# Two-layer trunk on one core: the memory tokens' keys and values computed in one pass over the contraction, with the keys a step behind

## The chip, the cores and the metric

The kernel runs on one core of one Trainium2 chip. The metric is the device time of one execution in microseconds (us); the time before is the median of three runs. Engines are named as the profile names them: PE (TensorE), PEld (its weight loads), ACT (ScalarE), DVE (VectorE), POOL (GpSimd) and SP (SyncE, which issues most of the DMAs).

## The reference, cut to what matters

Two layers (L = 2), 256 tokens, model width 2048, 256 memory tokens, float32. Each layer makes one input projection of `x`, runs three groups of heads on it, gates and concatenates them, projects the result and normalises. The change touches the part that reads the memory:

```
mkv = mem @ w_mem_kv                      # (256 x 2048) @ (2048 x 1024)
mk, mv = jnp.split(mkv, 2, axis=-1)       # keys and values, 512 columns each
...
y_m = memory_attention(heads_m(m_q), heads_m(mk), heads_m(mv))
...
return layer_norm(DEEPNORM_ALPHA * x + out, ln_g, ln_b)
```

`mem` is the same in both layers; `w_mem_kv` is not. The second layer's `x` is the first layer's result.

## The kernel before, in words

**Products in three parts.** Every float32 operand is split into a high part (ACT casts it to fp32r, line 117) and a low part (DVE subtracts, line 118); the helper `parts` does both. A product takes high·high, low·high and high·low. A cast therefore goes DMA, then ACT, then DVE, and PE needs all three.

**Pieces and quarters.** The contraction over 2048 is cut into 16 blocks of 128. Activations come in four *quarters* of 4 blocks (512 KB each; `load_quarter`, tile `x` from the pool `opp` with 5 buffers). Weights come in *pieces* of 512 KB (`piece`, tiles `raw`, `wh`, `wl`, 4 buffers each).

- `as_group` keeps the activations stationary and streams the weights: a piece is 2 blocks by 512 columns, 12 products of 512 columns. The memory's values (`G_MV`) are made so, in 8 pieces.
- `ws_group` keeps the weights stationary and streams the activations: two halves, each 4 pieces of 4 blocks by 256 columns, 16 products per piece (8 of 512 columns, 8 of 256). The memory's keys (`G_MK`) are made so, in 8 pieces that go over all four quarters twice; then the queries and keys of group B (`G_BQK`) from `x`.

**Order.** PE and SP follow the order in which the code is written (`manual_schedule`). ACT, DVE and POOL are ordered by a scheduler at build time; each then works strictly in that order. A pool gives a tile a buffer when its first writer is placed, in the order of the tiles. The heads are generators that `tick()` advances after each piece; the number that a generator yields is how many ticks it rests.

**The start of layer 0.** `begin_pieces` loads the memory's first two quarters and the first four pieces of the values in slices, all on SP's queue and all in `raw` buffers. Memory quarters 2 and 3 follow with `load_quarter`; the four quarters of `xT` are loaded inside `G_BQK`. The tile `res` (the residual, 2 MB) is not written before SP loads `xn` into it, after the second group of values of the heads.

**The start of layer 1.** `transposed` turns the residual into the four quarters of `x`, on PE: 8 groups of 4 transposes, one group after every second tick, each followed by a cast (ACT) and a subtraction (DVE) from a PSUM bank. It starts after the eight value pieces; `finish` runs off what is left. The memory's quarters of layer 1 are loaded and cast while the layer before is still in its output projection.

Of the kernel before, what the change touches and what calls it, by code (L numbers as in the profile page):

```python
# [8 lines left out]
F32 = mybir.dt.float32  # L9
F32R = mybir.dt.float32r  # L10
# [6 lines left out]
DVE = mybir.EngineType.DVE  # L17

P = 128
D = 2048  # L20
T = 256
# [11 lines left out]
G_MK, G_MV, G_BQK, G_AQ0, G_AK0, G_AQ1, G_AK1, G_MQ, G_BZ, G_AZ0, G_AZ1, G_MZ, G_WO = range(13)  # L33
AHEAD = 4000
# [3 lines left out]
def hybrid_trunk_kernel(  # L38
# [7 lines left out]
    pe, dve, act, pool, sp = nc.tensor, nc.vector, nc.scalar, nc.gpsimd, nc.sync  # L46
# [42 lines left out]
    def nm(s):  # L89
        uid[0] += 1  # L90
        return f"{s}_{uid[0]}"

    def mm(o, l, r, start, stop):
        pe.matmul(o, l, r, start=start, stop=stop, skip_group_check=True)  # L94
# [15 lines left out]
    def operand():  # L110

        x = opp.tile([P, 4, 2, T], F32R, name=nm("x"), tag="x")
        return x[:, :, 0], x[:, :, 1], x.rearrange("p j h t -> p j (h t)")

    def parts(hi, lo, src):

        act.copy(hi, src)  # L117
        dve.tensor_tensor(lo, src, hi.bitcast(F32), op=ALU.subtract)  # L118

    def load_quarter(src):  # L120

        with tc.high_priority(AHEAD):
            raw = wp.tile([P, 4, T], F32, name=nm("raw"), tag="raw")
            x = operand()
            sp.dma_start(raw, src)
            parts(x[0], x[1], raw)
        return x

    def piece(src, n, kp=2):

        with tc.high_priority(AHEAD):
            raw = wp.tile([P, kp, n], F32, name=nm("raw"), tag="raw")
            hi = wp.tile([P, kp, n], F32R, name=nm("wh"), tag="wh")
            lo = wp.tile([P, kp, n], F32R, name=nm("wl"), tag="wl")
            sp.dma_start(raw.rearrange("p k n -> p (k n)"), src)
            parts(hi, lo, raw)
        return hi, lo

    def begin_pieces(q, xsrc, wsrc):

        xraw = wp.tile([P, 4, T], F32, name=nm("raw"), tag="raw")
        x = operand()
        xh, xl, _ = x
        w = []
        for pc in range(2):
            wraw = wp.tile([P, 2, 512], F32, name=nm("raw"), tag="raw")
            wh = wp.tile([P, 2, 512], F32R, name=nm("wh"), tag="wh")
            wl = wp.tile([P, 2, 512], F32R, name=nm("wl"), tag="wl")
            w.append((wh, wl))
            for k in range(2):  # L150
                if q == 0 or k == 0:
                    j = slice(pc * 2 + k, pc * 2 + k + (1 if q == 0 else 2))
                    sp.dma_start(xraw[:, j], xsrc[:, j])  # L153
                    parts(xh[:, j], xl[:, j], xraw[:, j])
                cut = 2 if q == pc == k == 0 else 1
                for h in range(cut):
                    cs = slice(h * 512 // cut, (h + 1) * 512 // cut)
                    sp.dma_start(wraw[:, k, cs], wsrc[pc].rearrange("p (k n) -> p k n", k=2)[:, k, cs])  # L158
                    parts(wh[:, k, cs], wl[:, k, cs], wraw[:, k, cs])
        return x, w  # L160

    def ws_half(src, xq, first=None):

        acc = psd.tile([P, 2, 2, T], F32, name=nm("acc"), tag="acc")
        for pc in range(4):
            if first is not None:
                xq.append(load_quarter(first[pc]))
# [10 lines left out]
    def ws_group(src, xq, first=None):  # L178

        for half in range(2):  # L180
            acc = ws_half(src[half * 4:half * 4 + 4], xq, None if half else first)
            yield half * 2, acc[:, :, 0], acc[:, :, 1]

    def total(dst, a, b, scale=1.0):
        act.mul(dst, b, scale)  # L185
        dve.scalar_tensor_tensor(dst, a, scale, dst, op0=ALU.mult, op1=ALU.add)  # L186

    def as_products(o, t, xq, w, kt, kk):
        wh, wl = w
        xh, xl, _ = xq[kt // 4]  # L190
        j, ts = kt % 4, slice(t * P, (t + 1) * P)
        mm(o, xh[:, j, ts], wh[:, kk], kt == 0, False)
        mm(o, xl[:, j, ts], wh[:, kk], False, False)
        mm(o, xh[:, j, ts], wl[:, kk], False, kt == 15)

    def as_group(src, xq, n, kp=2, first=None, begin=False):

        acc = psd.tile([P, 2, 512], F32, name=nm("acc"), tag="acc")
        for pc in range(16 // kp):
            if begin and pc in (0, 2):  # L200
                x, ws = begin_pieces(pc // 2, first[pc // 2], src[pc:pc + 2])
                xq.append(x)
            if begin and pc < 4:
                w = ws[pc % 2]
            else:
                if first is not None and pc % 2 == 0:
                    xq.append(load_quarter(first[pc // 2]))
                w = piece(src[pc], n, kp)
# [258 lines left out]
    def transposed(xq):  # L467

        for q in range(4):
            x = operand()  # L470
            hi, lo, _ = x
            xq.append(x)
            for j in range(0, 4, 2):
                pt = bank()
                for jj in range(2):
                    kt = q * 4 + j + jj
                    for t in range(2):
                        pe.transpose(pt[:, jj * T + t * P:jj * T + (t + 1) * P], res[:, t, kt * P:(kt + 1) * P], ident)  # L478
# [31 lines left out]
    def norm_last(t, acc, stats, gb):  # L510

        with tc.manual_schedule(engines={DVE}):
# [14 lines left out]
            for n in range(5):  # L527
# [6 lines left out]
    res = per.tile([P, 2, D], F32, name="res")  # L534
    dve.memset(eps[:, 0:1], LN_EPS)
    dve.memset(eps[:, 1:2], RMS_EPS)

    attn = [per.tile([P, 4, P], F32, name=f"attn{par}") for par in range(2)]
    for l in range(L):
        mk = [per.tile([P, 4, T], F32R, name=nm("mk"), tag=f"mk{i}") for i in range(2)]  # L540
        mv = [per.tile([P, 2, 512], F32R, name=nm("mv"), tag=f"mv{i}") for i in range(2)]
        memq, xq = [], []
        parts(*mv, as_group(w512[l, G_MV], memq, 512, 2, memT, l == 0))
        if l:
            gens = [transposed(xq)]
            waiting.extend(gens)
        for i, a, b in ws_group(w512[l, G_MK], memq):
            tmp = scratch([P, 2, T])
            total(tmp, a, b)
            parts(mk[0][:, i:i + 2], mk[1][:, i:i + 2], tmp)  # L550
        if l:
            finish(gens)
# [187 lines left out]
```

## Time and profile before

| | |
|---|---|
| time, median of 3 runs | 949.04 us (947.6 to 949.91) |
| the profiled execution | 946.06 us, span 944.3 us, mean granted clock 0.993 |
| busy: PE, DVE, ACT, POOL | 923.1, 588.4, 498.8, 34.8 us |
| DMA | 178.70 MB, mean 189 GB/s |
| PE waits, 20 to 917 us | one of 0.5 us |

The span runs from the first to the last instruction. A row of the timeline reads: start, duration, engine, line, operation, written tile `<-` read tiles, shape, count; in brackets the engine's idle time before it and what ended it. Products are pipelined, so a row's duration is longer than its distance to the next row; the distance is what a product costs.

### The profile page before, as it was taken

The numbers are of one execution on the slowest core, as the hardware profiler recorded it, in microseconds if no ns is written. First come the engines' busy times: TensorE is split into PE (matmuls) and PEld (weight loads), VectorE is DVE, ScalarE is ACT, GpSimd is POOL, SyncE is SP. The second block draws the span as 40 slices with busy tenths as digits, with TensorE's granted clock in tenths as the row PEclk, the third lists the DMA queues.
The fourth block names the chain that finished last, engine by engine and source line by source line (L and its number), as shares of the span: only waits on it lengthen the run. The fifth ranks groups of instructions, "written<-read, shape, count | busy, mean of one in ns | idle before, by whom it ended". The sixth has DMA issues, their size and how long they took to land.

```text
span 944.3 us, 14493 instructions
## 1 busy us (share of the span) xinstructions
PE 923.1 (98%) x5684; PEld 819.4 (87%) x5684; DVE 588.4 (62%) x785; ACT 498.8 (53%) x714; POOL 34.8 (4%) x46
## 2 busy tenths in 40 slices
PE   7999999999999999999999999999999999999993
PEld 5889998898888888888988999889888888888893
DVE  5664487555565666555697445965555666565667
ACT  6554475376456655434555346635745576463341
POOL 1000000000000000000040000000000000010003
PEclk9999999999999999999999999999999999999997
DMA  8786855455554456765756465556555444676532
GB/s 273 248 271 182 295 191 173 150 182 166 190 165 162 158 180 196 251 199 183 242 187 214 142 210 181 188 161 190 159 183 177 158 156 157 201 240 206 197 114 89
DMA packets 54947, 178.70 MB, mean 189 GB/s; under 512 B 6336, under 2 KB 9952, under 8 KB 54624
## 3 DMA queue, kind: packets, MB, share of 16 engines
q1 hardware_dynamic: 53408, 173.56, 56.6%
q0 software_dynamic: 1472, 4.23, 1.9%
q8 instruction: 44, 0.72, 0.3%
q14 instruction: 23, 0.19, 0.1%
HBM read 175.67 MB, written 2.10 MB: 188 GB/s over the span
## 4 chain that ended last, share of the span: by engine, by line
PE 96%; DVE 2%; DMA 1%; issue 0%; SPq 0%; ACT 0%; DVEq 0%; ACTq 0%
PE acc L94 88%; PE bk L94 6%; DMA raw<-w 1%; DVE res L531 1%; PE bk L419 1%; DVE res L530 0%; PE bk L478 0%; PE bk L454 0%; DVE wl L118 0%; PE bk L390 0%; ACT wh L117 0%; SPq L158 0%; SPq L153 0%; PE bk L316 0%; DVE stats L488 0%
## 5 line engine op out<-in xcount | busy, mean ns | idle before, releaser
L118 DVE TENSOR_TENSOR wl<-raw,wh 128x1024 fp32r<-128x1024 f32 (+3 forms) x325 | 378.5, 1167 | 278.8 <-ACT wh L117 278.0
L117 ACT CAST wh<-raw 128x1024 fp32r<-128x1024 f32 (+3 forms) x325 | 323.2, 995 | 356.9 <-PE acc L94 256.2
L94 PE MATMUL acc<-x,wh 128*128 128x512 f32 x1408 | 505.2, 401 | 0.0
L94 PE MATMUL acc<-x,wl 128*128 128x256 f32 x1408 | 394.6, 280 | 0.0
L94 PE MATMUL acc<-wh,x 128*128 128x512 f32 (+2 forms) x1216 | 327.8, 354 | 4.9 <-ACT wh L117 4.9
L94 PEld LDWEIGHTS acc<-x,wh 128*128 128x128 f32 x1408 | 264.3, 188 | 60.4 <-issue 0.3
L94 PEld LDWEIGHTS acc<-x,wl 128*128 128x128 f32 x1408 | 266.0, 189 | 0.5
L94 PEld LDWEIGHTS acc<-wh,x 128*128 128x128 f32 x1216 | 219.2, 189 | 27.5 <-ACT wh L117 6.5
L94 PE MATMUL acc<-wl,x 128*128 128x512 f32 (+2 forms) x608 | 214.7, 353 | 0.5 <-DVE wl L118 0.5
L94 PEld LDWEIGHTS acc<-wl,x 128*128 128x128 f32 x608 | 115.0, 189 | 11.4 <-DVE wl L118 1.2
L118 DVE TENSOR_TENSOR x<-raw,x 128x1024 fp32r<-128x1024 f32 (+2 forms) x16 | 15.3, 956 | 14.9 <-ACT x L117 14.8
L411 ACT ACTIVATE sc<-sc,mx 128x128 f32<-128x128 f32 (+1 forms) x32 | 14.4, 450 | 17.8 <-DVE mx L409 17.7
L632 POOL DMA_DIRECT2D sc<-ln_g x8 | 4.3, 542 | 499.6 <-PE bk L94 439.1
L117 ACT CAST x<-raw 128x1024 fp32r<-128x1024 f32 (+2 forms) x16 | 13.3, 834 | 15.3 <-DMA raw<-memT 9.0
L186 DVE SCALAR_TENSOR_TENSOR sc<-acc,sc 128x512 f32<-128x512 f32 x24 | 16.4, 682 | 0.0
L404 DVE SCALAR_TENSOR_TENSOR sc<-bk,bias 128x384 f32<-128x384 f32 x16 | 8.9, 554 | 10.3 <-PE bk L94 10.3
L185 ACT ACTIVATE sc<-acc 128x512 f32<-128x512 f32 x24 | 14.3, 595 | 0.0
L621 DVE TENSOR_TENSOR sc<-sc,yr 128x512 f32<-128x512 f32 x16 | 11.0, 690 | 4.9 <-ACT sc L617 4.9
L94 PE MATMUL bk<-qk,qk 128*128 128x128 f32 (+1 forms) x64 | 13.1, 326 | 0.0
L94 PE MATMUL bk<-sc,asv 128*128 128x256 f32 (+1 forms) x64 | 13.0, 325 | 0.0
L487 DVE SCALAR_TENSOR_TENSOR res<-res,acc 128x512 f32<-128x512 f32 (+1 forms) x18 | 10.0, 595 | 4.5 <-PE acc L94 4.5
L617 ACT ACTIVATE sc<-sc 128x512 f32<-128x512 f32 x16 | 10.1, 630 | 4.6 <-DVE sc L186 4.5
(146 smaller groups left out, 515.7 us busy)
## 6 DMA issues: line engine op xcount, KB each, us to landing
raw<-w SPq DMA_DIRECT2D x252, 512.0 KB, 3.6
raw<-w SPq DMA_DIRECT2D x64, 388.0 KB, 3.1
raw<-memT SPq DMA_DIRECT2D x6, 512.0 KB, 4.1
bias<-relw SPq DMA_DIRECT2D x16, 192.0 KB, 3.6
raw<-xT SPq DMA_DIRECT2D x4, 512.0 KB, 4.5
res<-xn SPq DMA_DIRECT2D x1, 2048.0 KB, 9.0
sc<-ln_g POOLq DMA_DIRECT2D x8, 256.0 KB, 5.5
sc<-ln_b POOLq DMA_DIRECT2D x8, 256.0 KB, 5.7
```

The lines of the kernel that those rows point to most:

```text
L94: pe.matmul(o, l, r, start=start, stop=stop, skip_group_check=True)
L117: act.copy(hi, src)
L118: dve.tensor_tensor(lo, src, hi.bitcast(F32), op=ALU.subtract)
L185: act.mul(dst, b, scale)
L186: dve.scalar_tensor_tensor(dst, a, scale, dst, op0=ALU.mult, op1=ALU.add)
L404: dve.scalar_tensor_tensor(s, pb[:, :384], SCALE, bias[h], op0=ALU.mult, op1=ALU.add)
L411: act.activation(s[:, own[t]], s[:, own[t]], AF.Exp, bias=mx[:, t:t + 1], accum_out=zs[:, t:t + 1])
L419: pe.transpose(pt[:, i * P:(i + 1) * P], s[:, i * P:(i + 1) * P], ident)
L487: dve.scalar_tensor_tensor(r, r, ALPHA, acc, op0=ALU.mult, op1=ALU.add)
L531: dve.scalar_tensor_tensor(r, r, rstd, gb[n][1], op0=ALU.mult, op1=ALU.add)
L617: act.activation(sz, sz, AF.Silu)
L621: dve.tensor_tensor(sz, sz, yraw[i][:, j:j + 2], op=ALU.mult)
```

## The change

1. **One pass.** `memory_keys_values` replaces `as_group(G_MV)` and `ws_group(G_MK)`. In step p it makes value piece p (12 products) and then key piece p-1, which is now 2 blocks by all 512 columns (16 products into four PSUM blocks: two in an `acc` buffer, two in banks). Each memory quarter is used in three neighbouring steps and then released. Key pieces are read by two DMAs of 2 KB rows, each written as two runs of 1 KB.
2. **First loads.** In layer 0 the memory's slices go into `early`, a view of `res`, so that `raw` buffers serve weights alone. The first two slices are issued on ACT's queue. The quarters of `xT` follow into the same view, one in each of the steps 3, 5, 7 and 8 (`resident_quarter`). For pieces 0 and 1 the order on ACT and DVE is the written one.
3. **Zeros.** Before anything else PE multiplies a 128x128 tile of zeros by itself seven times.
4. **Layer 1.** `transposed` enters in step 3 instead of after the values, and rests one tick between groups instead of two, so its groups stand between value and key pieces.

```diff
+    def resident_quarter(q, src):
+        with tc.high_priority(AHEAD):
+            x = operand()
+            sp.dma_start(early[:, q], src)
+            parts(x[0], x[1], early[:, q])
+        return x
+
+    def first_piece(p, x, xsrc, wsrc):
+        wraw = wp.tile([P, 2, 512], F32, name=nm("raw"), tag="raw")
+        wh, wl = (wp.tile([P, 2, 512], F32R, name=nm(s), tag=s) for s in ("wh", "wl"))
+        xraw = early[:, p // 2]
+        j0 = p % 2 * 2
+        if p == 0:
+            for j in range(2):
+                act.dma_start(xraw[:, j:j + 1], xsrc[:, j:j + 1])
+            cuts = [(0, 0, 256), (0, 256, 512), (1, 0, 512)]
+        else:
+            sp.dma_start(xraw[:, j0:j0 + 2], xsrc[:, j0:j0 + 2])
+            cuts = [(0, 0, 512), (1, 0, 512)] if p == 1 else [(slice(0, 2), 0, 512)]
+        for k, c0, c1 in cuts:
+            sp.dma_start(wraw[:, k, c0:c1], wsrc.rearrange("p (k n) -> p k n", k=2)[:, k, c0:c1])
...
+    def memory_keys_values(l, mk, mv, each=None):
+        accv = psd.tile([P, 2, 512], F32, name=nm("acc"), tag="acc")
+        acck = psd.tile([P, 2, 2, T], F32, name=nm("acc"), tag="acc")
+        blocks = [acck[:, b] for b in range(2)] + [bank().rearrange("p (h t) -> p h t", h=2) for _ in range(2)]
+        for p in range(9):
+            if p < 8:
+                src = w512[l, G_MV, p]
...
+                    if p % 2 == 0:
+                        memq.append(load_quarter(memT[p // 2]))
+                    w = piece(src, 512)
+                for kk in range(2):
+                    for t in range(2):
+                        as_products(accv[:, t], t, memq, w, p * 2 + kk, kk)
+                if p == 7:
+                    parts(*mv, accv)
+                tick()
+            if each:
+                each(p)
+            if p:
+                p -= 1
+                wh, wl = piece([w512[l, G_MK, half * 4 + p // 2][:, p % 2 * 512:p % 2 * 512 + 512] for half in range(2)], 512)
...
+                        mm(blocks[b].rearrange("p h t -> p (h t)"), wh[:, kk, cs], both[:, j], p == kk == 0, False)
+                        mm(blocks[b][:, 1], wl[:, kk, cs], xh[:, j], False, p * 2 + kk == 15)
+                tick()
...
-                yield 2
+                yield 1
...
+    zeros = hd.tile([P, P], F32, name="zeros", tag="st")
+    dve.memset(zeros, 0.0)
+    idle = bank()
+    for _ in range(7):
+        mm(idle[:, :P], zeros, zeros, True, True)
...
-        parts(*mv, as_group(w512[l, G_MV], memq, 512, 2, memT, l == 0))
-        if l:
-            gens = [transposed(xq)]
-            waiting.extend(gens)
-        for i, a, b in ws_group(w512[l, G_MK], memq):
...
+        def each(p):
+            if l == 0 and p in (3, 5, 7, 8):
+                xq.append(resident_quarter(len(xq), xT[len(xq)]))
+            if l and p == 3:
+                gens.append(transposed(xq))
+                waiting.extend(gens)
+        memory_keys_values(l, mk, mv, each)
+        finish(gens)
...
-        for i, a, b in ws_group(w512[l, G_BQK], xq, None if l else xT):
+        for i, a, b in ws_group(w512[l, G_BQK], xq):
```

**Order on SP at the start.** First before, then now; `memT` is the memory, `w` the weights, `raw_100` and `raw_112` the first value piece, `raw_172` the first key piece.

```order
L153 DMA raw_98<-memT 128x256
L158 DMA raw_100<-w 128x256 x2
L153 DMA raw_98<-memT 128x256
L158 DMA raw_100<-w 128x512
L153 DMA raw_98<-memT 128x256
L158 DMA raw_118<-w 128x512
L153 DMA raw_98<-memT 128x256
L158 DMA raw_118<-w 128x512 [waits DMAHW0_49]
```

```order
L168 DMA raw_112<-w 128x256 x2
L168 DMA raw_112<-w 128x512
L165 DMA res<-memT 128x512
L168 DMA raw_145<-w 128x512 x2
L138 DMA raw_172<-w 128x2x256 [waits DMAHW0_49]
```

The two memory slices of 128x256 that stood at SP's head and third place are gone from it (they are ACT's first two instructions now, ahead of its table load), and the first half of key piece 0 is the ninth DMA of the two queues, behind 1536 KB.

**Order on ACT at the start of layer 1.** Before, then now, around the first cast of transposed columns. `x_4583` and `x_4564` are the first quarter of the layer's `x`, `x_4573` is the memory's third quarter (index 2), `wh_4659` the weights of key piece 4, `wh_4643` and `wh_4671` key pieces of before.

```order
L117 CAST wh_4643<-raw_4642 128x1024 [waits DMAHW3_49,PE_49,Activation_49]
L117 CAST mv_4391<-acc_4393 128x1024 [waits PE_49]
L117 CAST wh_4671<-raw_4670 128x1024 [waits DMAHW4_49,DVE_49,PE_49]
L117 CAST x_4583<-bk_4584 128x2x256 [waits PE_49]
L117 CAST wh_4701<-raw_4700 128x1024 [waits DMAHW5_49,DVE_49,PE_49]
```

```order
L117 CAST wh_4634<-raw_4633 128x1024 [waits DMAHW3_49,PE_49,Activation_49]
L117 CAST wh_4659<-raw_4658 128x1024 [waits DMAHW4_49,DMAHW5_49,PE_49,Activation_49]
L117 CAST x_4564<-bk_4565 128x2x256 [waits PE_49]
L117 CAST x_4573<-raw_4572 128x4x256 [waits DMAHW7_49]
L117 CAST wh_4695<-raw_4694 128x1024 [waits DMAHW7_49,DVE_49,PE_49]
```

Before, no memory quarter is cast here any more: the fourth was cast ahead of these rows. Now the third stands directly behind the cast of the first transposes, and that cast waits for PE. (The fourth, `x_4690`, stands in the same way behind the first transposes of the third quarter of `x`. On DVE the subtractions follow in the same order.)

**Order on PE at the same place.** Before, then now; `bk<-ident,res` are transposes, `wh_4578` is value piece 4, `wh_4592` a key piece, `bk_4412` the last block of key piece 2.

```order
L94 MATMUL acc_4560<-x_4395,wh_4562 128x512
L94 MATMUL acc_4560<-x_4395,wl_4563 128x256
L478 MATMUL bk_4584<-ident,res 128x128 [waits DMAHW3_49]
L478 MATMUL bk_4584<-ident,res 128x128 x3
L94 MATMUL acc_4560<-x_4436,wh_4592 128x512 [waits Activation_49]
L94 MATMUL acc_4560<-x_4436,wl_4593 128x256 [waits DVE_49]
```

```order
L94 MATMUL bk_4412<-x_4478,wl_4543 128x256
L529 MATMUL bk_4565<-ident,res 128x128 [waits DMAHW2_49,DVE_49]
L529 MATMUL bk_4565<-ident,res 128x128 [waits DMAHW3_49,DVE_49]
L529 MATMUL bk_4565<-ident,res 128x128 x2
L94 MATMUL acc_4409<-wh_4578,x_4573 128x512 [waits Activation_49]
L94 MATMUL acc_4409<-wh_4578,x_4573 128x512 [waits DVE_49]
L94 MATMUL acc_4409<-wl_4579,x_4573 128x512
```

Value piece 4, the first to use the memory's third quarter `x_4573`, now follows the first transposes directly; its first product waits for ACT and its second for DVE.

More of the change, by code (lines that the diff above doesn't have):

```diff
@@ L134, in piece @@
             lo = wp.tile([P, kp, n], F32R, name=nm("wl"), tag="wl")
-            sp.dma_start(raw.rearrange("p k n -> p (k n)"), src)
+            if isinstance(src, list):
+                w = n // len(src)
+                for i, part in enumerate(src):
+                    sp.dma_start(raw[:, :, i * w:(i + 1) * w], part.rearrange("p (k n) -> p k n", k=kp))
+            else:
+                sp.dma_start(raw.rearrange("p k n -> p (k n)"), src)
             parts(hi, lo, raw)
         return hi, lo
[L139 to L160, printed above, removed]
@@ L162, in ws_half @@
-    def ws_half(src, xq, first=None):
+    def resident_quarter(q, src):
[9 more added lines that the diff above has]
+        j0 = p % 2 * 2
+        cuts = []
+        if p == 0:
+            for j in range(2):
+                act.dma_start(xraw[:, j:j + 1], xsrc[:, j:j + 1])
+            cuts = [(0, 0, 256), (0, 256, 512), (1, 0, 512)]
+        else:
+            sp.dma_start(xraw[:, j0:j0 + 2], xsrc[:, j0:j0 + 2])
+            cuts = [(0, 0, 512), (1, 0, 512)] if p == 1 else [(slice(0, 2), 0, 512)]
+        for k, c0, c1 in cuts:
+            sp.dma_start(wraw[:, k, c0:c1], wsrc.rearrange("p (k n) -> p k n", k=2)[:, k, c0:c1])
+        with tc.manual_schedule(engines={DVE, mybir.EngineType.Activation}) if p < 2 else tc.high_priority(AHEAD):
+            if p:
+                parts(x[0][:, j0:j0 + 2], x[1][:, j0:j0 + 2], xraw[:, j0:j0 + 2])
+            for k, c0, c1 in cuts:
+                if p == c0 == 0:
+                    parts(x[0][:, k:k + 1], x[1][:, k:k + 1], xraw[:, k:k + 1])
+                parts(wh[:, k, c0:c1], wl[:, k, c0:c1], wraw[:, k, c0:c1])
+        return wh, wl
@@ L176, in ws_half, with ws_group @@
         return acc
-    def ws_group(src, xq, first=None):
+    def ws_group(src, xq):
         for half in range(2):
-            acc = ws_half(src[half * 4:half * 4 + 4], xq, None if half else first)
+            acc = ws_half(src[half * 4:half * 4 + 4], xq)
             yield half * 2, acc[:, :, 0], acc[:, :, 1]
@@ L194, in as_products, with as_group @@
         mm(o, xh[:, j, ts], wl[:, kk], False, kt == 15)
-    def as_group(src, xq, n, kp=2, first=None, begin=False):
+    def as_group(src, xq, n, kp=2):
         acc = psd.tile([P, 2, 512], F32, name=nm("acc"), tag="acc")
         for pc in range(16 // kp):
[L200 to L208, printed above, removed]
+            w = piece(src[pc], n, kp)
             for kk in range(kp):
```

31 lines of the change are left out of this document (23 added, 8 removed).

## The prediction

> **What bounds the kernel now.** I read the page first, then the chain of waits in order of time, then the timelines of the two places that the change rewrites: the first 20 us, and the start of layer 1.
>
> ```profile
> PE 923.1 (98%) x5684; PEld 819.4 (87%) x5684; DVE 588.4 (62%) x785; ACT 498.8 (53%) x714; POOL 34.8 (4%) x46
> ```
>
> ```profile
> 3.54 3.86 DMA raw<-w
> ...
> 8.17 3.47 DMA raw<-w
> ...
> 13.03 4.38 DMA raw<-w
> ...
> 19.88 91.98 PE acc L94 x506
> ```
>
> ```profile
> PE acc L94 <- DVE wl L118: 0.5, 1, 0.5
> ```
>
> ```profile
> 491.85 0.44 PE bk L478 x4
> 492.29 5.56 PE acc L94 x32
> ...
> 510.46 2.78 PE acc L94 x16
> 513.24 1.75 PE bk L478 x16
> 514.99 5.09 PE acc L94 x29
> ```
>
> PE is the bound. Up to 19.88 us the chain runs through transfers and casts: PE is short of data. The third fence is the list of PE's waits from 20 to 917 us, whole: one wait of 0.5 us, which ends at its very start. The last fence is the chain at layer 1: transposes (0.44 us a group) stand between products without a gap. So only the first 20 us and the tail can become shorter, and the tail is not touched; everywhere else a new wait of PE adds its full length.
>
> **The start.** PE's lag at a time is that time less the work done.
>
> ```profile
> 4.47 1.22 PE L94 MATMUL acc<-wh,x 128*128 128x512 f32 x2 [4.47 <-ACT wh L117]
> 5.49 0.63 PE L94 MATMUL acc<-wl,x 128*128 128x512 f32 x1
> 5.91 1.05 PE L94 MATMUL acc<-wh,x 128*128 128x512 f32 x2
> 9.40 0.54 PE L94 MATMUL acc<-wl,x 128*128 128x512 f32 x1
> 477.99 0.62 PE L94 MATMUL acc<-wh,x 128*128 128x512 f32 x2
> 478.67 0.39 PE L94 MATMUL acc<-wh,x 128*128 128x512 f32 x1
> ```
>
> From 477.99 to 478.67 three products start, so one costs 0.227 us and a value piece of 12 costs 2.72; the key piece at 510.46 takes 2.78. At the beginning a product costs 0.42 (5.49 to 5.91), up to about 9.4. When PE resumes for good at 19.88 it has done 50 products, 11.33 us: a lag of 8.55 us.
>
> ```profile
> 0.74 0.38 SPq L153 DMA_DIRECT2D raw<-memT  x1
> 1.18 0.90 SPq L158 DMA_DIRECT2D raw<-w  x2
> 2.59 0.44 SPq L158 DMA_DIRECT2D raw<-w  x1
> 6.43 0.62 ACT L117 CAST wh<-raw 128x512 fp32r<-128x512 f32 x1 [0.46 <-DMA raw<-w]
> 11.66 0.62 ACT L117 CAST wh<-raw 128x512 fp32r<-128x512 f32 x1 [0.45 <-DMA raw<-w]
> ```
>
> ```profile
> 2.00:4.00 2.00, 0.00 (x0) 0.00 (x0) 0.43 (x1) 0.83 (x3) 1.99 (x4) 1.00 0.86 229
> 5.00:8.00 3.00, 3.00 (x8) 2.00 (x7) 1.35 (x3) 1.91 (x5) 0.00 (x0) 1.00 1.03 367
> 15.00:18.50 3.50, 3.13 (x14) 2.25 (x12) 1.94 (x3) 2.17 (x3) 0.00 (x0) 1.00 1.00 387
> ```
>
> The last two columns of the windows are the DMA engines' busy share and GB/s: 229 in 2 to 4 us, where rows of 1 KB move, 367 with rows of 2 KB, 387 with rows of 4 KB. The first 768 KB (two memory slices, value piece 0) are cast at 6.43, five queue entries after the first. With two slices on ACT's queue the last of them goes out as SP's third entry, about 0.97 us earlier (1.62 for 2.59): they land at 5.46. Then 768 KB at 367 GB/s (2.14 us) and key piece 0, 524,288 bytes in runs of 1 KB, at 229 GB/s (2.29): 9.9. The key piece's second product needs its low part, a cast and a subtraction later:
>
> ```profile
> L118 DVE TENSOR_TENSOR wl<-raw,wh 128x1024 fp32r<-128x1024 f32 x252 | 310.9, 1237 | 203.3 <-ACT wh L117 202.8
> L117 ACT CAST wh<-raw 128x1024 fp32r<-128x1024 f32 x252 | 264.1, 1049 | 271.5 <-PE acc L94 182.8 <-issue 65.4 <-DMA raw<-w 17.8
> ```
>
> 9.9 + 1.05 + 1.24 = 12.2 us, with 25 products (5.67 us) done: a lag of 6.5, a gain of 2.0. Later key pieces have more lead: a step needs 1280 KB and gives PE 5.5 us. Bounds: if key piece 0 comes no sooner than the row at 11.66, the half of a piece behind about as many bytes (low part at 13.0), the gain is 1.2; if it comes at 387 GB/s, PE's own 24 products decide (start 4.4, a clock slow until about 6), and the gain is at most 3.4. I take 2.0, from the two windows.
>
> A rule weighed against a row: the Trainium skill, "DMA: Bandwidth & Descriptors", Specifications, gives 512 B as the least transfer for line rate. By it runs of 1 KB would cost what others do, key piece 0 would land 0.9 us earlier, and the sum would end near 953. The windows above (229 against 387 GB/s, though the first holds the queue's start) speak against it.
>
> **The zeros** cost nothing: they start when DVE has cleared the tile, near 1 us.
>
> ```profile
> 231.55 0.66 PE bk L94 x4
> 0.74 1.28 ACT L117 ACT_TABLE_LOAD   x1 [0.74 <-PEq L730]
> ```
>
> The engines start at 0.74. 384 float32 columns take 0.66 us, so seven times 128 take 1.5, or 2.9 at the slow start's 0.42 for 0.227: done before 4.47, when PE gets its first data. ACT's two DMA issues (0.44 each) push its table load (1.28) to 2.9, just ahead of the first slice: 0. The zeros gain nothing either in my sum: 24 products are done by 12.2 even if the clock rises only at 9.4. That is their cover; without it they would be worth up to 1 us.
>
> **Layer 0's end.** The queries of group B now wait for the value accumulator's buffer. Its cast stands behind two weight casts and the last `xT` quarter, whose DMA waits on SP until the memory's last slices are cast, with key piece 7 behind it. From the end of value piece 7 this takes about 1.05 + 3 x 1.14 + 1.24 = 5.7 us if the data came just then, and covered are two key pieces, 5.6. Cost 0.2; 0 if data comes earlier, 1.5 if four transfers go at 229 GB/s.
>
> **Layer 1.** Here the order decides. ACT casts the memory's third quarter behind the first transposed columns, and value piece 4 needs it right after those transposes; the same holds for the fourth quarter and value piece 6.
>
> ```profile
> 472.73 1.05 ACT L117 CAST x<-raw 128x1024 fp32r<-128x1024 f32 x1 [0.26 <-DMA raw<-memT]
> 473.69 1.04 ACT L117 CAST wh<-raw 128x1024 fp32r<-128x1024 f32 x1
> 493.50 0.58 ACT L117 CAST x<-bk 128x512 fp32r<-128x512 f32 x1
> 494.97 1.21 DVE L118 TENSOR_TENSOR mv<-acc,mv 128x1024 fp32r<-128x1024 f32 x1
> 496.11 1.33 DVE L118 TENSOR_TENSOR wl<-raw,wh 128x1024 fp32r<-128x1024 f32 x1
> 497.36 0.68 DVE L118 TENSOR_TENSOR x<-bk,x 128x512 fp32r<-128x512 f32 x1
> 497.96 2.35 DVE L118 TENSOR_TENSOR wl<-raw,wh 128x1024 fp32r<-128x1024 f32 x2
> 491.69 4.66 POOL L505 TENSOR_TENSOR res<-res,sc 128x512 f32<-128x512 f32 x3
> ```
>
> Count from the end of key piece 2. PE: transposes to 0.44. ACT: the weights of key piece 4, whose buffer key piece 2 just gave back, from 0.05; next cast 0.96 later (472.73 to 473.69): transposed columns at 1.0, the memory quarter at 1.5, done at 2.55. First product at 2.6, so PE idled 2.16. DVE: low weights from 1.1, columns at 2.25 (1.14 later), done and free at 2.85 (0.60 later), the quarter's low part until 4.07; second product at 4.1. PE idled 1.27 more. Together 3.4 us, and 6.8 at the two places. Floor: had the weights been cast before, the columns start at 0.65 and the second product at 3.5, 2.8 us idle each, 5.7 together. Behind PE nothing else waits that could hide it, and no slack follows. I take 6.8, since the order puts the weights first; top 7.0.
>
> The transposes themselves only move: POOL, the last writer of `res`, ends at 496.3 in this trace, when the groups now stand at 486 to 505, and the columns that a group reads come earlier than the last ones (the first quarter's on DVE alone). Eight more key DMAs per layer cost SP 0.44 each, 3.5 us over 44, while it mostly waits for buffers; two more small sums per layer go to ACT and DVE, which idle 47% and 38%. `xn` is loaded into `res` long after `early` is read. All these: 0.
>
> **Sum:** -2.0 + 0.2 + 6.8 = +5.0 us. The profiled execution took 946.06 (1.8 around its span of 944.3) and should become 951.1; the median stands 3.0 above it, so 949.04 + 5.0 = 954.0.
>
> **Rivals.**
> - *The clock falls in the two waits.* At the tail:
>
> ```profile
> 928.00:929.00 1.00, 0.60 (x5) 0.39 (x4) 1.00 (x2) 0.00 (x0) 1.00 (x2) 1.00 0.00 0
> 929.00:931.00 2.00, 0.00 (x0) 0.00 (x0) 2.00 (x4) 0.00 (x0) 0.32 (x1) 1.00 0.45 179
> 931.00:932.00 1.00, 0.00 (x0) 0.00 (x0) 1.00 (x4) 0.00 (x0) 0.00 (x0) 0.65 1.01 369
> ```
>
>   PE ends at 928.6, and the granted clock (column before the DMA's) is halved near 931.3, after 2.7 us. My wait is 3.66 us long with one product in it. If it halves, products cost 0.42 for a while; the slow start lasted 4.9 us, which loses up to 2.4 each time: 956.4 for one, 958.8 for two. Against it: neither part alone reaches 2.7. The Trainium skill, "TensorE: Matmul & The Clock Gate", HAM oscillation, allows gaps up to about 3.4 us in a free-running window; by it only an unlucky phase would be hit. The row halves sooner. Chance 0.26.
> - *Transfers bound the one pass of layer 0.* At 229 GB/s for key pieces a step costs 1.35 + 0.68 + 2.29 = 4.3 us of DMA and 5.7 with an `xT` quarter, against 5.5 for PE; four such steps and a queue stopped at the last quarter give 2 us: 956. For it: the runs of 1 KB; against: some 4 us of lead. Chance 0.08.
> - *Both terms at their ends*, gain 3.4, waits 5.7: +2.3, 951.3, within 0.3% (2.85 us; about what a measurement of this kernel tells from no change). Chance 0.10.
> - *Faster:* the start's gain stands alone, 946 to 947, if value pieces 4 and 6 find their quarters cast. It decides in the start's favour only where each wait stays under 0.3 us; the order on ACT speaks against it. Chance 0.04.
>
> **Numbers.** The forecast has 0.52. Slower: 0.52 + 0.26 + 0.08 = 0.86; same 0.10; faster 0.04. Range from 951.3 (both ends) to 957.5 (one fall of the clock and the top of the waits).
>
> **What would show it.** Start: PE steady from about 12 us, the last wait there ended by DVE's `wl`. Layer 1: two pairs of waits of PE, about 2.2 us for ACT's `x` and 1.3 for DVE's `x`, near 488 and 504; after each, products at 0.227 us, or at 0.42 if the clock fell. Layer 0 near 50 us: a wait under 0.3. PE's count 14 higher. Wrong if the waits at layer 1 are missing, or if PE still stalls after 20 us in layer 0.

## The result, and the profile after

The changed kernel took 960.68 us (median of 4 runs, 959.78 to 961.34) against 949.17 for the kernel before (4 runs, 947.6 to 949.91): a ratio of 1.0121, 95% interval 1.0107 to 1.0135. It is 11.5 us slower; forecast were 5.0, with a range that ended at 957.5. The profiled execution took 959.78 us, its span is 957.5 (before: 946.06 and 944.3).

The page of the changed kernel, engines and slices; a digit is a tenth of a slice of 23.9 us, `PEclk` the granted clock of TensorE (PE):

```profile
PE 930.1 (97%) x5698; PEld 823.4 (86%) x5698; DVE 588.5 (61%) x787; ACT 498.0 (52%) x715; POOL 35.6 (4%) x46
PE   8999999999999999999978999999999999999993
PEclk9999999999999999999989999999999999999997
```

PE is busy 7.0 us longer (923.1 before) and idle 6.2 us longer. 3.4 of the 7.0 are the zeros. Two slices, the 21st and 22nd, stand out, and the first of them has a lower clock: 479 to 527 us, the start of layer 1. The list of PE's waits from 442 to 540 us is two rows:

```profile
PE acc L94 <- ACT x L117: 6.0, 2, 4.0
PE acc L94 <- DVE x L118: 2.8, 2, 1.7
```

Total, count, longest. These are the two places that the prediction named. On PE's timeline (brackets: the idle time ahead of the row and what ended it):

```profile
489.63 0.70 PE L94 MATMUL acc<-wh,x 128*128 128x512 f32 x1 [3.99 <-ACT x L117]
492.05 0.79 PE L94 MATMUL acc<-wh,x 128*128 128x512 f32 x1 [1.72 <-DVE x L118]
492.64 0.63 PE L94 MATMUL acc<-wl,x 128*128 128x512 f32 x1
493.07 1.05 PE L94 MATMUL acc<-wh,x 128*128 128x512 f32 x2
...
509.10 0.49 PE L94 MATMUL acc<-wh,x 128*128 128x512 f32 x1 [2.01 <-ACT x L117]
510.67 0.80 PE L94 MATMUL acc<-wh,x 128*128 128x512 f32 x1 [1.07 <-DVE x L118]
```

From 492.64 to 493.07 one product takes 0.43 us, not 0.227. The windows show why; the column between POOL and the DMA's two is the granted clock:

```profile
489.00:490.00 1.00, 0.37 (x1) 0.20 (x1) 1.00 (x1) 0.57 (x1) 1.00 (x2) 0.88 0.79 217
490.00:496.00 6.00, 4.28 (x10) 3.14 (x10) 2.00 (x3) 0.00 (x0) 3.16 (x4) 0.50 0.71 214
496.00:497.00 1.00, 1.00 (x6) 0.75 (x5) 0.00 (x0) 0.28 (x1) 0.00 (x0) 0.71 0.02 8
```

The second place has the same picture from 510 to 514. To see where the 13.2 us between the two spans lie, the same marks are compared: the first copy of the attention values (ACT, `asv<-acc`), the first `add_residual` of layer 0's third output column group (DVE, at 444.25 before and 442.74 after), the sum of `gq` in layer 1 (ACT, 527.00 and 539.62) and PE's last product.

| mark | before | after | difference | grown since |
|---|---|---|---|---|
| first copy of the values, layer 0 | 93.4 | 91.9 | -1.5 | -1.5 |
| third column group, layer 0 | 444.25 | 442.74 | -1.5 | 0 |
| sum of `gq`, layer 1 | 527.00 | 539.62 | +12.6 | **+14.1** |
| last product | 928.60 | 941.43 | +12.8 | +0.2 |
| end of span | 944.3 | 957.5 | +13.2 | +0.4 |

All of the loss but 0.6 us lies between the third and the fourth row of this table. One window over that stretch, of before and then of after (the second number is PE's busy time):

```profile
444.25:527.00 82.75, 82.75 (x519) 74.64 (x518) 64.27 (x77) 44.55 (x52) 12.79 (x10) 1.00 0.62 202
```

```profile
442.74:539.62 96.88, 88.09 (x519) 77.13 (x518) 64.28 (x78) 44.65 (x54) 13.55 (x10) 0.95 0.56 172
```

The same 519 matmul records; 8.8 us of idle time and 5.3 us more of busy time, in which the mean clock is 0.95.

### The profile page after: what moved, and what is told of

Its sections match the earlier page's. It is cut to its first block, busy times and chain, and to the rows that moved or that the text cites. A ratio compares the mean times of both kernels' runs of the same rounds, so it can differ in the third digit from the quotient of the medians.

```text
span 957.5 us, 14560 instructions
## 1 busy us (share of the span) xinstructions
PE 930.1 (97%) x5698; PEld 823.4 (86%) x5698; DVE 588.5 (61%) x787; ACT 498.0 (52%) x715; POOL 35.6 (4%) x46
## 5 line engine op out<-in xcount | busy, mean ns | idle before, releaser
L118 DVE TENSOR_TENSOR wl<-raw,wh 128x1024 fp32r<-128x1024 f32 (+2 forms) x323 | 378.7, 1174 | 299.6 <-ACT wh L117 298.3
L117 ACT CAST wh<-raw 128x1024 fp32r<-128x1024 f32 (+2 forms) x323 | 322.8, 1000 | 376.9 <-PE acc L94 275.4
L94 PE MATMUL acc<-x,wh 128*128 128x512 f32 x1344 | 484.2, 402 | 0.0
L94 PE MATMUL acc<-x,wl 128*128 128x256 f32 x1344 | 376.8, 280 | 0.3 <-DVE wl L118 0.3
L94 PEld LDWEIGHTS acc<-x,wh 128*128 128x128 f32 x1344 | 252.4, 188 | 57.7 <-issue 0.3
L94 PEld LDWEIGHTS acc<-x,wl 128*128 128x128 f32 x1344 | 253.9, 189 | 1.5 <-DVE wl L118 0.7
L94 PE MATMUL bk<-x,wh 128*128 128x512 f32 x64 | 24.1, 398 | 0.0
L94 PE MATMUL bk<-x,wl 128*128 128x256 f32 x64 | 18.0, 281 | 0.0
L94 PEld LDWEIGHTS bk<-x,wh 128*128 128x128 f32 x64 | 12.0, 188 | 3.0
L118 DVE TENSOR_TENSOR x<-res,x 128x512 fp32r<-128x512 f32 (+2 forms) x13 | 10.5, 810 | 4.4 <-ACT x L117 4.3
```

## The experiments

Ratios are to the kernel before, measured in turn with each on the same chip; the changed kernel's is 1.0121.

**Both waits taken away.** Pool order is the supposed cause: a memory quarter's buffer comes behind a transposed tile's, so its cast does too. The edit loads the second to fourth quarter of layer 1 one value step earlier, which puts the buffers of the third and fourth ahead of those transposed tiles, and changes nothing else. That the data itself came too late is a rival that the changed kernel's trace excludes: the DMAs of the third and fourth quarter went out at 468.34 and 485.19 and such a DMA lands within 4.7 us, but ACT cast them at 488.53 and 508.01.

```
-                    if p % 2 == 0:
-                        memq.append(load_quarter(memT[p // 2]))
+                    if p == 0 or p in (1, 3, 5):
+                        memq.append(load_quarter(memT[(p + 1) // 2]))
```

> In layer 1 the memory's quarters 1, 2 and 3 are loaded one value step earlier (steps 1, 3 and 5), so that quarter 3's buffer comes ahead of the first transposed tile in the pool and quarter 4's ahead of the third; everything else is the changed kernel. Theory (the two places in layer 1 where TensorE waits for a memory quarter's casts, 5.7 and 3.1 us, and the halved clock behind each, cost what the change lost): both waits go and the granted clock stays at 1.00 from 480 to 530 us. The last copy of the attention values stood 12.8 us later than before; without 8.8 us of waits and some 4 us of slow clock it stands where it stood before, so about 949 us (947.5 to 951). Rival (the transposes between the passes' pieces, or the pass itself, cost the time, and the waits only show it): another wait of 3 us or more shows between 480 and 530 us, and the time stays above 955. Rival (the clock falls by the load on the chip, not by the waits): waits go, clock still shows windows near 0.5, 953.

947.48 us (11 runs, 947.03 to 947.99), ratio 0.9988 (0.9977 to 0.9998). Its list of PE's waits from 440 to 540 us, whole, and a window:

```profile
PE bk L529 <- DVE x L118: 0.7, 1, 0.7
```

```profile
490.00:500.00 10.00, 9.32 (x54) 7.78 (x53) 9.23 (x10) 5.79 (x8) 3.67 (x4) 1.00 0.78 242
```

The two waits and the slow clock are gone and with them 1.3% of the time. The transposes stand at the same steps as in the changed kernel, so it was not they that cost. The pass over k as such costs 0.8 us: from the third column group to `gq` PE is busy 83.58 us here, with the clock at 1.00, and 82.75 before.

**One of the two taken away.** `if l and p == 3` becomes `if l and p == 4`: quarter 3 then comes ahead of the transposes, quarter 4 not.

> The transposes of layer 1 enter after value step 4 instead of 3, one edit of one digit. Quarter 3's buffer then comes ahead of the first transposed tile, quarter 4's still behind the third. Theory: the first place (5.7 us of wait and its slow clock of some 2.5 us) is gone, the second place stays with 3.1 to 3.5 us of wait in two pieces and 1.5 us of slow clock: about 953 us (951.5 to 955). Rival (the wait is not the pool's order but the transposes' own work beside a busy DVE): the first wait moves a step later and stays over 4 us, 958 or more.

955.77 us (5 runs, 954.23 to 956.69), ratio 1.0077 (1.0064 to 1.009), above the expected range. The first place is gone; what is left there is a wait of 0.7 us for DVE's `wl` at 488.98. The second stayed, and larger than I expected:

```profile
502.24 0.80 PE L94 MATMUL acc<-wh,x 128*128 128x512 f32 x1 [3.52 <-ACT x L117]
503.80 0.79 PE L94 MATMUL acc<-wh,x 128*128 128x512 f32 x1 [0.77 <-DVE x L118]
```

4.3 us instead of 3.1. ACT had the key piece's weights only at 499.71, waiting for their DMA (the columns stood ready at 498.7). So the size of the wait is not a constant of the order; it depends on how late transfers are running.

**The waits kept, filled with work.** Zeros are multiplied into the values' accumulator ahead of and behind the first product of value pieces 4 and 6.

```
+                fill = {4: (16, 6), 6: (7, 4)}.get(p, (0, 0)) if l else (0, 0)
+                for _ in range(fill[0]):
+                    mm(accv[:, 0, :P], zeros, zeros, False, False)
```

> The changed kernel with zeros multiplied into the values' accumulator inside the two waits of layer 1: 16 products of 128 columns ahead of value step 4's first product and 6 behind it, 7 and 4 at step 6 (one such product of the start took 0.48 us at half clock, so an estimated 0.24 at full: 3.8, 1.4, 1.7 and 1.0 us against waits of 4.0, 1.7, 2.0 and 1.1). They add zero, so that the sums stay. Theory (the idle stretch lowers the clock, and the slow products behind it are a price of its own beside the wait): the granted clock stays at 1.00 through both places, the real products behind them take 0.23 us instead of 0.43, and the kernel is 3.5 to 4.5 us faster than the changed one: 956.5 us (955.5 to 957.5), the waits still there but filled. Rival (the clock falls for another cause, such as the burst of DMA and ACT work at that place, or products with zeros do not hold it): 960 to 962, the clock at 0.5 as in the changed kernel.

956.25 us (5 runs, 955.61 to 957.11), ratio 1.0085 (1.0073 to 1.0098): 0.36% of the time, 3.4 us, below the changed kernel by the ratios, 4.4 by the medians. PE at the first place, and the window behind it:

```profile
485.87 3.74 PE L94 MATMUL acc<-zeros 128*128 128x128 f32 x32
489.89 0.50 PE L94 MATMUL acc<-wh,x 128*128 128x512 f32 x1 [0.28 <-ACT x L117]
490.22 1.50 PE L94 MATMUL acc<-zeros 128*128 128x128 f32 x12
492.46 0.50 PE L94 MATMUL acc<-wh,x 128*128 128x512 f32 x1 [0.74 <-DVE x L118]
```

```profile
493.00:496.00 3.00, 3.00 (x17) 2.51 (x16) 0.00 (x0) 0.94 (x1) 0.58 (x2) 1.00 0.76 237
```

The real products start when they did, within 0.4 us, for the same releasers, and the clock stays at 1.00. So the clock is a price of its own, about 4 us, that idle time sets off and not load, and products with zeros avert it.

**POOL left out of the norm.** In the trace of the changed kernel the cast of quarter 3 stands behind the key piece's weights, which came late: ACT, then SP, DVE and POOL of the changed kernel:

```profile
487.10 1.04 ACT L117 CAST wh<-raw 128x1024 fp32r<-128x1024 f32 x1 [3.80 <-DMA raw<-w]
488.05 0.58 ACT L117 CAST x<-bk 128x512 fp32r<-128x512 f32 x1
488.53 1.05 ACT L117 CAST x<-raw 128x1024 fp32r<-128x1024 f32 x1
```

```profile
483.51 0.88 SPq L138 DMA_DIRECT2D raw<-w  x2
```

```profile
481.16 6.20 DVE L118 TENSOR_TENSOR wl<-raw,wh 128x1024 fp32r<-128x1024 f32 x3
488.18 2.09 DVE L118 TENSOR_TENSOR wl<-raw,wh 128x1024 fp32r<-128x1024 f32 x1 [0.81 <-ACT wh L117]
```

```profile
479.61 4.47 POOL L555 TENSOR_TENSOR res<-res,sc 128x512 f32<-128x512 f32 x3 [93.14 <-DMA raw<-w]
```

A subtraction takes 2.07 us there and 1.23 elsewhere; it holds a raw buffer for as long, SP waits for that buffer, and the DMA goes out at 483.5. The edit removes POOL's two operations in `norm_between`, so this kernel leaves out gain and bias in the rows that POOL has.

> The changed kernel without POOL's eight multiplications and additions of the norm between the layers (the second half of the rows in four of five column groups stays without gain and bias; that part of the computation is left out). Theory (DVE's subtraction of a key piece takes 2.07 us instead of 1.23 while POOL works on the residual, so raw buffers come free later, the weights of key piece 4 are issued late at 483.5, and quarter 3's cast stands behind them): the subtractions in 479 to 492 us take about 1.23 us, the first place's wait falls from 5.7 to about 3.4 us, the second stays at 3.1: 2.3 us less, 958.4 us (957.4 to 959.4), a little lower if the clock also falls for a shorter time. Rival (the stretch of DVE is its own reading of the residual or the DMA, not POOL): 2.07 us stays and the time too, 960.7. Rival (the late DMA is what counts and it is late for SP's order): subtractions short, wait still above 5 us.

957.5 us (4 runs, 957.31 to 958.02), ratio 1.0098 (1.0084 to 1.0112). DVE and then PE:

```profile
481.96 2.39 DVE L118 TENSOR_TENSOR wl<-raw,wh 128x1024 fp32r<-128x1024 f32 x2 [0.83 <-ACT wh L117]
```

```profile
487.49 0.49 PE L94 MATMUL acc<-wh,x 128*128 128x512 f32 x1 [2.05 <-ACT x L117]
489.05 0.50 PE L94 MATMUL acc<-wh,x 128*128 128x512 f32 x1 [1.07 <-DVE x L118]
505.58 0.50 PE L94 MATMUL acc<-wh,x 128*128 128x512 f32 x1 [2.01 <-ACT x L117]
507.15 0.79 PE L94 MATMUL acc<-wh,x 128*128 128x512 f32 x1 [1.06 <-DVE x L118]
```

The subtractions are back at 1.20, and both places wait 3.1 us, close to the prediction's count from the order (2.16 and 1.27 were forecast). The other 2.6 us of the first place came from POOL; the way through DVE, a buffer, SP and a DMA is read from the changed kernel's trace, where SP waited 5.8 us for a subtraction ahead of the DMA at 483.51. Without POOL's work that DMA goes out at 481.16.

**The start.** Two kernels with the quarters ahead: without the zeros, and with nine of them.

> The kernel with the quarters ahead, without the zeros that TensorE multiplies first. By the prediction's term (zeros cost and bring 0): 947.5 us as with them (946.8 to 948.2). By the trace of the changed kernel (products at 0.23 us from 5.3 on, where the kernel before had them at 0.43 until about 9.4): some ten first products take 0.2 us more, 2 us, of which the waits at 8.65 and 12.49 (1.0 us together) swallow half: 948.5 (948.0 to 949.5). A difference under 0.3 us speaks for the prediction's zero.

> The kernel with the quarters ahead, with nine products of zeros at the start instead of seven: by 0.48 us each they end at about 5.4 instead of 4.4, and the first real product, which came at 4.9 to 5.4, follows without idle time. Theory (in the profile of the kernel with the quarters ahead 1.0 us of idle time behind the zeros left the products at 0.43 us until about 9.5, in that of the changed kernel 0.5 us did not): products at 0.23 us from the first on, 0.3 to 0.8 us less: 946.9 us (946.5 to 947.3). Rival (the start is bound by transfers and casts, so that a faster first product only waits later): 947.5, or 0.4 more if the zeros end behind the first operands.

947.72 us (12 runs), ratio 0.9989 (0.9981 to 0.9998), and 947.86 (12 runs), 0.9991 (0.9982 to 1.0001); with seven 947.48. The first real products without zeros, and then with nine:

```profile
4.82 1.22 PE L94 MATMUL acc<-wh,x 128*128 128x512 f32 x2 [4.82 <-ACT wh L117]
...
13.07 0.39 PE L94 MATMUL acc<-x,wl 128*128 128x256 f32 x1 [0.28 <-DVE wl L118]
```

```profile
5.23 0.73 PE L94 MATMUL acc<-wh,x 128*128 128x512 f32 x2 [0.44 <-ACT wh L117]
...
9.41 0.73 PE L94 MATMUL acc<-wh,x 128*128 128x512 f32 x2 [1.14 <-ACT wh L117]
...
13.27 0.39 PE L94 MATMUL acc<-x,wl 128*128 128x256 f32 x1 [0.35 <-DVE wl L118]
```

A pair takes 0.73 us behind the zeros and 1.22 without them: the zeros do raise the clock. But a faster PE then waits 1.1 us at 9.41, and both reach the key piece's low part at about 13.2. That also answers my own expectation of +1.0 for leaving the zeros out, which was wrong: the first 13 us are bound by transfers and casts. The zeros alone, put into the kernel before:

> The kernel before with the zeros alone. The prediction put the zeros at 0. Theory: the first products run at 0.23 us some 4 us earlier, but the layer's first pieces wait for transfers and casts, so that TensorE only waits later: 948.5 like before (947.5 to 949.0), and a wait or two of 0.5 to 1.5 us in the first 20 us that the kernel before does not have. Rival: 1 to 2 us faster, 947. Its layer 1 is that of the kernel before: a wait of TensorE for DVE between 485 and 500 us in its profile would show what the profile of before missed.

948.97 us (12 runs, 948.18 to 951.96), ratio 1.0002 (0.9991 to 1.0012): nothing, as the prediction had it. Its profiled execution, at 951.96 the longest of the twelve, showed something else. Layer 1 is that of the kernel before, and PE, DVE and windows there read:

```profile
493.13 0.39 PE L94 MATMUL acc<-x,wl 128*128 128x256 f32 x1 [2.78 <-DVE wl L118]
```

```profile
484.29 7.12 DVE L508 SCALAR_TENSOR_TENSOR res<-res,rstd,sc 128x512 f32<-128x512 f32 x6
491.33 7.32 DVE L118 TENSOR_TENSOR wl<-raw,wh 128x1024 fp32r<-128x1024 f32 x4
```

```profile
494.00:497.00 3.00, 3.00 (x11) 2.56 (x10) 3.00 (x3) 0.00 (x0) 3.00 (x3) 0.51 0.85 198
```

So the kernel before probably has a wait of its own here in some executions, by the same stretched DVE, and a fall of the clock behind it. Its own profile does not show it: that is of the execution of 946.06, the shortest of all.

**One pass in layer 0 alone.** Layer 1 computes values and then keys as before.

> The one pass over k in layer 0 alone; layer 1 computes values and then keys as in the kernel before, with the transposes beside the keys. Start, zeros, first activations and layer 0 are the changed kernel's. Theory (in layer 1 the change only costs: waits, slow clock, and about 0.1 us at each of 8 changes from a key piece to a value piece, where two products take 0.55 us instead of 0.46): no waits and no slow clock in layer 1, and 0.8 to 1.0 us less than with the quarters ahead: 946.6 us (945.8 to 947.3). Rival (the changes between pieces cost nothing that the end sees): 947.5 like the kernel with the quarters ahead.

947.42 us (12 runs, 946.03 to 950.27), ratio 0.9989 (0.9977 to 1.0001): no better than the quarters ahead, where I expected 0.9 less. Its lowest runs are 1 us under the other's lowest, its highest 2 us above, and its profile has the wait of the row above at 490.31 with 1.89 us. In that execution the old order lost in layer 1 what it saves there.

**Half of the filling.** `{4: (16, 0), 6: (0, 4)}`.

> The filled kernel with half of the filling: at the first place only the wait for ACT (4.0 us) is filled with zeros and the one for DVE (1.7) left, at the second only the one for DVE (1.1) is filled and the one for ACT (2.0) left. Theory 1 (the clock falls only where idle time of some 3 us comes together, as in 3.1 us with one product inside): a single wait of 1.7 or 2.0 us leaves the clock at 1.00 and the time is that of the filled kernel, 956.3 (955.5 to 957). Theory 2 (any wait of about 2 us lowers it): the clock shows 0.5 windows at both places, some 3.5 us more, 959.8 (958.5 to 961). One place of the two: 958.

958.11 us (6 runs), ratio 1.0099 (1.0083 to 1.0115); the profiled execution alone took 954.22. In that one PE waited 2.01 us at 505.44, right ahead of filled time, and the clock stayed at 1.00; the wait for DVE that was to be left at the first place had shrunk to 0.3. The other five took 957.5 to 958.8, so that something happened in them that the profile does not have, probably a fall of the clock; that is not shown. It is inconclusive for single waits.

**The norm on DVE.** `LN_POOL[0]` is emptied, so that DVE does all of the norm between the layers, in three kernels: before, one pass in layer 0 alone, and quarters ahead.

> The kernel before, with the norm between the layers computed by DVE alone: POOL's eight multiplications and additions on the residual move to DVE (four more pairs, some 0.55 us each operation, 4.5 us in all, against subtractions of key pieces that take about 2 us instead of 1.2 beside POOL, and DVE's own part of the norm that takes 0.9 to 1.2 us instead of 0.6). Theory (the kernel before loses 2 to 3 us in most of its executions to a wait of TensorE for DVE's stretched subtractions at the start of layer 1, which its profiled execution of 946.06 happened not to show, since its median stands 2.5 to 3 above that): median 946.3 (945.5 to 947), its times within 1 us of each other. Rival (the spread of the kernel before comes from its start or from the chip): 948.5 as before, with the same spread. Rival (DVE with all the norm is itself late): 949 or more.

> One pass in layer 0 alone, and the norm between the layers on DVE alone. With one pass in layer 0 alone the times lay between 946.0 and 950.3 and its profile shows one wait of 1.9 us of TensorE for DVE at 490.3. Theory: that wait goes, and the times gather at the lower end: 945.3 (944.5 to 946.3). Rival (the spread is the start's): 947.4, spread unchanged.

> The kernel with the quarters ahead and the norm on DVE alone. It has only one wait of 0.7 us in layer 1 (transposes for DVE), which should go; the 0.1 us at each change from a key piece to a value piece stays: 946.8 (946.0 to 947.5). If DVE becomes late with the norm, 948 or more.

948.37 us, ratio 0.9991 (0.9982 to 1.0); 947.59, ratio 0.9978 (0.9969 to 0.9987); 946.87 (10 runs, 946.0 to 948.0), ratio 0.9977 (0.9968 to 0.9986). In the first two a wait for DVE remains, a little earlier, at 483.29 (0.85 us) and 482.31 (1.66): with the norm added, DVE is itself late there. The expected 946.3 and 945.3 were missed; that wait is one reason. But the times above 949.2 are gone (15 of the 34 runs of the kernel before were above that). With the quarters ahead no wait is left after 13 us; the whole list is

```profile
PE bk L94 <- DVE eps L595: 1.1, 1, 1.1
PE acc L94 <- ACT wh L117: 0.6, 2, 0.5
PE acc L94 <- DVE wl L118: 0.3, 1, 0.3
```

This is the fastest version: 0.23% below the kernel before and 1.4% below the changed kernel. One pass in layer 0 alone with the same norm comes to the same within the noise; with the quarters ahead alone, with or without zeros, the gain is about 0.1%.

## Why the prediction was wrong

The direction, the two places, their releasers and the two parts of each wait were right. Two terms failed, and one step of the sum.

- **The clock, a rival with a chance of 0.26, belonged into the sum.** I argued that neither part of a wait alone reaches 2.7 us. But a single product between two idle stretches (0.49 us in the rows) did not save the clock: it fell at both places, also where the parts were only 2.05 and 1.07 us. The filled kernel gives its price, about 4 us for the two. Of the 5.3 us of longer busy time 0.8 is not the clock's, as the quarters-ahead kernel shows (83.58 against 82.75 us). Value products in triples take 0.69 to 0.70 us in the one pass and 0.68 before, 0.4 us for 32 triples; the rest probably lies where a value piece follows a key piece and its first pair takes 0.55 us instead of 0.46 (486.24 to 486.79 in that kernel).
- **The first wait, 3.4 us forecast, 5.7 measured.** The count from the order is nearly right (3.1 with POOL left out). It assumed that the key piece's weights are cast as soon as their buffer is free. Their cast began 1.5 us after PE had begun to wait, since their DMA was late. I had quoted POOL's row at 491.69 and DVE's 2.35 us for two subtractions, but left out the row ahead of them, where DVE needed 7.92 us for four beside POOL. This is DVE before:

```profile
487.13 7.92 DVE L118 TENSOR_TENSOR wl<-raw,wh 128x1024 fp32r<-128x1024 f32 x4
```

  The second place, where POOL is done, took 3.1.
- **Median and profile.** I added the change to the median, 3.0 us above the profiled execution. Those 3 us are no constant: the changed kernel's median stands 0.9 above its profile. So profile to profile the change costs 13.7 us, median to median 11.5. Why the profile of before is so far below its median stays open. Part lies in the start: the kernel before with the norm on DVE, which is the same program up to that norm, has its first copy of the values at 94.50 and not at 93.38. A wait for DVE at layer 1's start, like the 2.78 us with the zeros alone, may account for the longest executions. That most of them have it is not shown: without POOL in that norm the ratio fell only to 0.9991.
- **The start: -2.0 forecast, -1.5 measured at the first mark.** The last wait is the key piece's low part, as forecast, and comes at 12.49 with 25 products done: a lag of 6.8 us against 8.55 before, a gain of 1.7; the subtraction ahead of it was 0.3 us later than counted. These are single executions: kernels with the same start have the first mark between 91.67 and 92.71, and the kernel before at 93.38 or 94.50, so the gain is known to about 1 us either way. One reading in this term was wrong, and that it did no harm was luck. I took 229 GB/s as the price of runs of 1 KB. On ACT of the changed kernel value piece 2 and key piece 1 are cast as their DMAs land:

```profile
12.09 1.05 ACT L117 CAST wh<-raw 128x1024 fp32r<-128x1024 f32 x1 [0.40 <-DMA raw<-w]
13.58 1.05 ACT L117 CAST wh<-raw 128x1024 fp32r<-128x1024 f32 x1 [0.44 <-DMA raw<-w]
```

  The 524,288 bytes of the key piece in runs of 1 KB follow in 1.49 us, an estimated 350 GB/s. So the 229 belong to the first microseconds and not to the length of the runs. The first key piece landed near the forecast 9.9 all the same (its cast began at 10.12): from 5 to 8 us the changed kernel moved 308 GB/s, less than the 367 that I had put in. The Trainium skill's rule that I had weighed against it ("DMA: Bandwidth & Descriptors", Specifications: full rate from 512 B) agrees with this.
- **Zeros 0:** right, by two kernels. **Layer 0's end, +0.2:** 0, no wait. **Transfers as the bound of layer 0:** did not happen. **Transposes and additional DMAs, 0:** right; the quarters-ahead kernel has them all at 947.48.

Both weak terms lie in the waits of layer 1: how long the first one is, and what the clock does behind each. Corrected by the runs the sum reads -1.5 + 8.8 + 5.3 + 0.6 = 13.2 us of span.

## What to carry to other kernels

A wait of the bounding engine is priced with the clock behind it: where TensorE's idle stretches add to about 3 us with only a product or two between them, as at the places here, count the products of the next 3.4 or 6.8 us at half speed. When a count from the order of instructions says how long a wait is, look at each producer's rows just ahead of that place for anything that is stretched or late, for a queue that runs behind turns a wait of 3 us into one of 4 to 6. And before the work is blamed for a wait, try the pool's order and allocate one step earlier: here that single edit returned all that was lost.

## What was not expected of the hardware

- The granted clock fell after idle time of 2.78 us in one piece, and after 2.05 + 1.07 and 2.01 + 1.06 us with one product between. It stayed after 1.66, 1.89 and 2.01 us. It fell 2.5 to 4.1 us after the idle time began and stayed low for 3.41 us at three places and for 6.83 at three. These times have an order. In the changed kernel it fell at 489.76, rose at 496.58, fell at 510.24 and rose at 513.65: steps of two, four and one times 3.41 us. In all 14 traces the changes of the clock lie on such a grid. In the grid step before each of the six falls in layer 1 PE was busy for at most 0.98 us; in all other steps from the first rise to PE's last product that had the clock at 1.00, for at least 1.75. Two steps of the changed kernel and one of the zeros alone, each with a fall at its end, and one of one pass in layer 0 alone with the norm on DVE, where the clock stayed (the second number is PE's busy time):

```profile
486.34:489.76 3.42, 0.13 (x1) 0.13 (x1) 2.61 (x2) 2.48 (x3) 3.42 (x3) 1.00 0.79 219
506.82:510.24 3.42, 0.77 (x4) 0.22 (x2) 2.59 (x3) 2.23 (x3) 0.00 (x0) 1.00 0.46 146
```

```profile
490.63:494.04 3.41, 0.91 (x5) 0.82 (x6) 3.41 (x3) 1.31 (x2) 3.41 (x3) 1.00 0.00 0
```

```profile
479.09:482.50 3.41, 1.75 (x8) 1.13 (x8) 3.41 (x6) 1.06 (x1) 0.00 (x0) 1.00 0.16 17
```

  So in these traces it is the work within a grid step that decides, and not the length of one gap; whether a wait of 2 to 3 us costs the clock would then depend on where it lies on the grid. No run shows where the edge lies between 0.98 and 1.75 us. The Trainium skill, "TensorE: Matmul & The Clock Gate", HAM oscillation, forbids idle gaps above about 3.4 us. The traces agree on the size but not on the edge: shorter gaps sufficed here, and one product inside a gap did not save the clock.
- Multiplying zeros counts as work for that clock, inside a wait (with them no grid step of layer 1 has less than 2.40 us of PE work, where the changed kernel has 0.13) and at the start. At the start seven zeros were not always enough: the first pair took 1.22 us again with 1.0 us of idle time behind the zeros (kernel with the quarters ahead), but also with 0.17 us (zeros alone), so the idle time alone does not explain it. At the start the column of the granted clock reads 1.00 while products take 0.42 us, so there only the durations tell.
- DVE's subtraction of two SBUF tiles took 2.07 us beside POOL's multiplications and additions and 1.20 without them. The Trainium skill, "GPSIMD Engine Reference", Specifications, says that POOL shares its SBUF interfaces with VectorE and contends with instructions of two SBUF inputs. The trace agrees, and the prediction should have drawn on it. One subtraction of a memory quarter took 1.21 us at 490.79 although POOL's row still ran, so that not each one is hit.
